# Dense expert pass: the residual parts of the expert weights formed on GpSimd instead of VectorE

## The chip, the cores and the metric

One Trainium2 chip, one of its cores. The metric is the device time of one execution of the whole program in microseconds (us). The engines are named as in the profile: PE (TensorE), DVE (VectorE), ACT (ScalarE), POOL (GpSimd), SP (SyncE, which here only issues transfers).

## The reference

One layer of a diffusion backbone: a mixer (gated MLP and a bidirectional recurrence) and then a channel mixer that picks experts. The change lies in the channel mixer, for 1152 tokens (128 of a prompt, 1024 of a sample), 16384 experts of one neuron each, and 128 chosen experts for each token:

```python
def block(args):
    xb, ib, gb = args
    ue = jnp.take(u_tab, ib, axis=0)
    ve = jnp.take(v_tab, ib, axis=0)
    a = jax.nn.gelu(jnp.einsum('bd,bed->be', xb, ue)) * gb
    return jnp.einsum('be,bed->bd', a, ve)
```

`ib` are the indices of the chosen experts, `gb` their weights (a softmax), `u_tab` and `v_tab` are tables of 16384 rows of 1024 float32. Behind it come a gated residual and a last norm.

## The kernel before

The tokens lie in nine tiles of 128. After the mixer and the choice of experts, two methods share the tiles. Five tiles (640 tokens) are **dense**: they meet every expert, and a weight matrix that is zero for the experts not chosen does the picking. Four tiles are done **row by row**: for each token the rows of its 128 experts are fetched. One of these four is done earlier; the other three go beside the dense pass, as work that fills the engines.

**The dense pass** runs over 128 expert tiles `e` of 128 experts (`for e in range(129)`; its last round only finishes). For each of them:

- SP loads a tile of `u` (`ur`, 128x1024, 512 KB) and one of `v` (`vr`) into one of three buffers with the tag `raw` (`load_split`).
- TensorE multiplies float32 numbers as two parts of a rounded type (float32r): a first part H = round(x), made by ACT as a copy (line 99), and a second part L = x - H, made by DVE as a subtraction (line 100, helper `split`). A product then takes three matmuls: H by H, H by L, L by H (lines 129 to 131, `mmx`). So `ur` becomes `uH`, `uL`, two buffers each, and `vr` becomes `vH`, `vL`, five buffers each.
- `hidden` (lines 977 to 981): 48 matmuls of 320 columns give the activations of the 640 tokens in PSUM (`pH`), and ACT applies the GELU into `a`.
- DVE multiplies `a` by the weights `Gt` (line 1062), and `a` is split into `aH` (ACT) and `aL` (DVE).
- `out_res`: 18 matmuls of 512 columns add this expert tile's part to the sums of three token tiles, which stay in PSUM (`pout`). For the other two token tiles `out_rot` does four expert tiles at a time: 48 matmuls into two PSUM buffers (`prot`, shared with `pH`), and DVE adds each of the four results to a sum in SBUF (`accd`, line 1045).

**The rows** (`gather`): POOL issues an indirect transfer of 128 rows, one for each token of the tile (`gu`, line 795, or `gv`, line 808; 512 KB each), and DVE uses it: line 798 is the product and sum with the token (`jk`), line 813 adds a scaled row to the result (`acc`). The fetched rows have six buffers (four and two more); a fetch waits on POOL until DVE has freed one. 768 rows of this kind (3 tiles, 128 of `u` and 128 of `v` each) are done in the dense pass.

What sets the order: each engine works its instructions off in one order, fixed when the program is built. The rows are advanced from the function `fill`, which stands behind every split and every addition to `accd`: 16 times for four expert tiles, 1.525 rows each time. `anchor` and `paced` keep a row's DVE instruction behind the main stream's instruction that was handed to `fill` two calls ago (`KEEP` = 2). The choice of a tile's experts (`combine_late`, line 119 on DVE) is worked in as well, a little before its rows.

```python
    def paced(ins):
        if anchors:
            tc.add_manual_dep(ins.ins, anchors[0].ins.name,
```

Of the kernel before, what the change touches and what calls it, by code (L numbers as in the profile page):

```python
# [20 lines left out]
NT = 9            # token tiles of 128: tile 0 is the prompt, 1..8 the sample  # L21
NS = 8
EPS = 1e-6
CF = {}           # slots of [128, 512] and of [128, 1024] in the pool of a phase
NGR = 4           # slots of fetched rows, and those that the dense pass adds
# [7 lines left out]
AH = (1, 2)       # of how many blocks of one-hots ScalarE does the weighting  # L33
# [4 lines left out]
TB = 32           # tokens of a block of the weight matrix in DRAM  # L38
OT = 4            # tokens of a block of one-hots
GI = 4            # expert tiles of one load of the weights  # L40
# units of 128 x 1024 weights in the stream
U_ZI, U_HG, U_GR = 0, 4, 16
GATHER = [0, 1, 2, 3]                             # token tiles whose experts are fetched row by row
DENSE = [5, 6, 7, 8, 4]                           # token tiles that meet every expert
ND = len(DENSE)
TD = 128 * ND
RES = 3                                           # dense tiles whose sums stay in PSUM
# [4 lines left out]
def hybrid_kernel(ctx, tc, x_all, pos, c2t, w_ada, b_ada, wst, wspt, bsp, lbraw, vecs, fng, skt, state,  # L52
# [16 lines left out]
    gate_d = dram.tile([4, D], F32, name="gate_d")      # gate1 (ctx, lat), gate2 (ctx, lat)  # L69
# [12 lines left out]
    vec = consts.tile([128, 24], F32, name="vec")        # g1(8) g2(8) sgu(4) hgrn(4), channel on partition  # L82
# [6 lines left out]
    lb = consts.tile([128, 3, 8], F32, name="lb")        # lb, (1-lb)/2, (1+lb)/2  # L89

# [7 lines left out]
    def split(src, H, L):  # L98
        A.activation(H, src, AF.Copy)  # L99
        return V.tensor_tensor(out=L, in0=src, in1=H.bitcast(F32), op=OP.subtract)  # L100
# [3 lines left out]
    def anchor(ins, keep):  # L104
        """the filling work on VectorE queues behind the main stream's instruction `keep` anchors ago"""
        anchors.append(ins)
        while len(anchors) > keep:
            anchors.popleft()
# [15 lines left out]
    def mmx(ps, a, b, first, last):  # L124
        """a.T @ b for operands in one float32 part or in two float32r parts"""
        if len(a) == 1:
            P.matmul(ps, a[0], b[0], start=first, stop=last)
        else:
            P.matmul(ps, a[0], b[0], start=first, stop=False)  # L129
            P.matmul(ps, a[0], b[1], start=False, stop=False)  # L130
            P.matmul(ps, a[1], b[0], start=False, stop=last)  # L131
# [4 lines left out]
    def rap(t, off, dims):  # L136
        """free-dim pattern on a tile"""
        a = t[:]
        return bass.AP(tensor=a.tensor, offset=a.offset + off, ap=[list(a.ap[0])] + dims)

# [9 lines left out]
    # work that fills the engines beside the main stream: generators, advanced a step at a time  # L150
# [42 lines left out]
    # order of the six modulation vectors: shift1 scale1 gate1 shift2 scale2 gate2  # L193
# [30 lines left out]
    def norm_T(pool, xn, which, cnd, parts, back=None):  # L224
        """transposes normalised tiles, applies scale and shift, stores the parts; back(k, full) sees
        the whole float32 value"""
        n = len(xn)
        T = n * 128
        for k in range(8):
            pt = ptp("pnt")  # L230
            for i in range(n):
                P.transpose(pt[:, i * 128:(i + 1) * 128], xn[i][:, k * 128:(k + 1) * 128], ident)
            if len(parts) == 1:
                full = parts[0][:, k, :]
            else:
                full = pool.tile([128, 512], F32, name="full", tag="h512", bufs=CF['h512'])
            A.activation(full[:, 0:T], pt[:, 0:T], AF.Identity, scale=aT[:, which, k, cnd:cnd + 1],
                         bias=modT[:, 2 * which, k, cnd:cnd + 1])
            if len(parts) == 2:
                split(full, parts[0][:, k, :], parts[1][:, k, :])  # L240
            if back is not None:
                back(k, full)
# [25 lines left out]
    def proj_rows(u0, opd, n, evac, native, half=None):  # L268
        """token-major product with a 512 wide block (4 units); opd(k): parts [128, T]; evac(i, psum)"""
# [16 lines left out]
    def hgrn(pool, blocks, proj, vsrc, states):  # L286
        """blocks: (token tile, head) of each 128 columns; proj(j, evac): products for q, fw, bw"""
        NB = len(blocks)
        NTOK = NB * 128
        K2 = pool.tile([128, 2, NTOK], F32, name="K2")       # fw, bw  # L290
        Q2 = pool.tile([128, 2, NTOK], F32, name="Q2")       # bw, fw
        F2 = pool.tile([128, 2, NTOK], F32, name="F2")       # fw, bw
# [27 lines left out]
        for lev in range(7):  # L320
            w = 1 << lev
            Kc = pool.tile([128, NTOK], F32, name="Kc", bufs=1)   # even segments forward, odd ones backward
# [11 lines left out]
            # K: fw first halves by the total of the second, bw second halves by the total of the first  # L334
# [8 lines left out]
            # totals of the doubled segments: the second level in T2, the others in place of the gates  # L343
# [7 lines left out]
        T128 = tbase                                        # F2[:, d, T128 + block]  # L351
# [63 lines left out]
    def combine(gp, t, tv, ti, al=None, c4=None, V=V, h0=0, h1=8, res=None):  # L415
        """the 16 best sums of a head: products of the two lists, with (i+1)(j+1) <= 16"""
# [28 lines left out]
        if res is None:  # L445
            res = al("res", 384).rearrange("p (a b) -> p a b", a=3)    # i1, i2, g
# [3 lines left out]
        hk = lambda x: x[:, :, None, :].to_broadcast(SH)                     # over the list position  # L450
        lp = lambda x: x[:, :, :, None].to_broadcast(SH)                     # over the chosen
# [26 lines left out]
        # softmax over the 16 of a head  # L478
# [16 lines left out]
        else:  # L495
# [3 lines left out]
            rt = gp.tile([128, 2, 128], F16, name="rt", bufs=4)      # i2, i1  # L499
            V.tensor_copy(rt, pt[:, 0:256].rearrange("p (a b) -> p a b", a=2))  # L500
            rg = gp.tile([128, 128], F32, name="rg", bufs=4)         # g (scaled)
            V.tensor_scalar(rg, pt[:, 256:384], 16384.0, None, op0=OP.mult)
            gl = gp.tile([128, 2, 128], F16, name="gl", bufs=4)      # its float16 part, what is left
# [4 lines left out]
    def build_G(gp, i, rt, rg, gl, tags):  # L508
        SH = [128, 2, 128, OT]

        def one_hots(t0):
            o4 = gp.tile([128, 4, 128 * OT], F16, name="oh", tag="c4", bufs=3)
            oh = o4[:, 0:2].rearrange("p a (j t) -> p a j t", t=OT)          # of i2, of i1
            og = o4[:, 2].rearrange("p (t j) -> p t j", t=OT)                # of i1, weighted
# [40 lines left out]
    def group(gp, tiles, hpar, native):  # L555
# [21 lines left out]
        yparts = 2 if tiles is GA else 1                 # the second parts lie where the other group builds  # L577
# [25 lines left out]
        # y_a  # L603
# [32 lines left out]
        # merge, channel on partition (twice the merge: the half goes into the gate)  # L636
# [21 lines left out]
        # out projection and residual  # L658
# [26 lines left out]
        else:  # L685
            advance(choose_q, 10000)
            advance(build_q, 10000)
            # two tiles a part
# [23 lines left out]
        for i in range(n):  # L712
            # the dense tiles wait in DRAM for the dense pass
            if tiles[i] in DENSE:
                c0 = DENSE.index(tiles[i]) * 128
                for z in range(2):
                    for kh in range(2):
                        nc.sync.dma_start(h2T_d[z][:, kh * 4:kh * 4 + 4, c0:c0 + 128],
                                          h2[z].a[kh][:, :, i * 128:(i + 1) * 128].bitcast(F32))
        # queries, scores, top 16 of each half  # L720
# [27 lines left out]
        for i in range(n):  # L748
            t = tiles[i]
            if tiles is GB and t in GATHER:  # L750
                # looked at in the dense pass
# [70 lines left out]
    def final(pool, t, dst, src, x1, gt2, fg):  # L822
        """residual, last norm, store; src: the retrieved sum in column blocks"""
# [12 lines left out]
    # ================= program =================  # L836
# [4 lines left out]
    # left side: a slot for the transposed tokens, and the pool of the row by row retrieval  # L841
# [6 lines left out]
    # lower bound: first row of softmax over the two rows, channel on partition: [128, (dir, head)]  # L848
# [13 lines left out]
    # -- the prompt, token tile 0  # L862
# [42 lines left out]
    # the half of the position embedding that depends on the column is the same for every tile  # L905
# [32 lines left out]
    # -- HGRN over the sample; its tiles in the order of the columns of the two groups  # L938
# [21 lines left out]
    # -- the sample in two groups  # L960
# [21 lines left out]
    # the first expert tiles meet the tokens while the last choice is worked out  # L982
# [23 lines left out]
    def fill(ins):  # L1006
        """fetched rows; the choice of a tile's experts a little before the rows of the one before it end"""
        anchor(ins, KEEP)
# [11 lines left out]
    def load_split(src, nm, bufs):  # L1020
# [3 lines left out]
        fill(split(raw, H, L))  # L1024
# [23 lines left out]
    for e in range(129):  # L1048
        if e < 128:
# [12 lines left out]
            V.tensor_tensor(out=ab, in0=ab, in1=Gt[:, :, e % GI, :], op=OP.mult)  # L1062
# [43 lines left out]
def _layout(ins):  # L1106
    f = lambda n: np.ascontiguousarray(np.asarray(ins[n], dtype=np.float32))

    def tu(w, c0):                   # 128 output channels, all of the contraction: [p, k, 128]
# [3 lines left out]
    def nu(w, c0):                   # 512 output channels as 4 units [p, 2, 512]  # L1113
# [73 lines left out]
```

## Time and profile before

| | |
|---|---|
| runs of the kernel, median of 3 | 3696.43 us (3687.48 to 3701.36) |
| span of the profiled execution | 3697.6 us |
| PE busy | 3351.2 us, 91% |
| PEld (weight loads) | 2757.2 us, 75% |
| DVE busy | 2840.2 us, 77% |
| ACT busy | 1157.4 us, 31% |
| POOL busy | 1440.8 us, 39% |
| mean DMA rate | 263 GB/s over the span |

The profiled execution's own time is known by its span, which is what the sums here are made against; it lies 1.2 us above the median of the runs. The dense pass takes the second half of the span: the first matmul into `pout` starts at 1784 us, the last addition to `accd` at 3675.7 us. In the table a busy share is a mean over all stages; what matters for the change is the share in the dense pass, and how often one engine there waits for another.

### The profile page before, as it was taken

The numbers are of one execution on the slowest core, as the hardware profiler recorded it, in microseconds if no ns is written. First come the engines' busy times: TensorE is split into PE (matmuls) and PEld (weight loads), VectorE is DVE, ScalarE is ACT, GpSimd is POOL, SyncE is SP. The second block draws the span as 40 slices with busy tenths as digits, with TensorE's granted clock in tenths as the row PEclk, the third lists the DMA queues.
The fourth block names the chain that finished last, engine by engine and source line by source line (L and its number), as shares of the span: only waits on it lengthen the run. The fifth ranks groups of instructions, "written<-read, shape, count | busy, mean of one in ns | idle before, by whom it ended". The sixth has DMA issues, their size and how long they took to land. (4 is left out here: it accounts for less than half of the span.)

```text
span 3697.6 us, 48818 instructions
## 1 busy us (share of the span) xinstructions
PE 3351.2 (91%) x17547; PEld 2757.2 (75%) x17547; DVE 2840.2 (77%) x5427; ACT 1157.4 (31%) x2075; POOL 1440.8 (39%) x1128
## 2 busy tenths in 40 slices
PE   7787889899797899888789999889999989999997
PEld 3265678777476676576688989788888878898996
DVE  1315698787499987588787889888888888888888
ACT  2511233432222387735322222222222222222222
POOL 0100632265311220000255554556555465655664
PEclk9899999999898999888799999999999999999998
DMA  7676854488842476441798898889988799989986
GB/s 267 226 272 208 297 189 153 158 292 307 296 161 97 163 278 252 172 165 75 257 327 307 316 335 286 311 298 330 326 308 316 256 327 338 318 301 328 328 313 249
DMA packets 361957, 971.12 MB, mean 263 GB/s; under 512 B 32721, under 2 KB 142673, under 8 KB 356081
## 3 DMA queue, kind: packets, MB, share of 16 engines
q0 software_dynamic: 149824, 546.37, 41.6%
q1 hardware_dynamic: 211888, 421.62, 33.1%
q8 instruction: 138, 2.26, 0.2%
q14 instruction: 107, 0.87, 0.1%
HBM read 897.07 MB, written 70.80 MB: 262 GB/s over the span
## 5 line engine op out<-in xcount | busy, mean ns | idle before, releaser
L795 POOL DMA_INDIRECT gu<-in_urow_dram,ix x512 | 693.5, 1354 | 1024.8 <-DVE jk L798 368.8
L808 POOL DMA_INDIRECT gv<-in_vrow_dram,ix x512 | 694.7, 1357 | 720.6 <-DVE acc L813 388.2
L798 DVE SCALAR_TENSOR_TENSOR jk<-gu,h2r 128x1024 f16<-128x1024 f32 x512 | 624.9, 1220 | 125.0 <-DMA gu<-in_urow_dram,ix 118.7
L813 DVE SCALAR_TENSOR_TENSOR acc<-gv,act,acc 128x1024 f32<-128x1024 f32 x508 | 651.3, 1282 | 65.9 <-DMA gv<-in_vrow_dram,ix 57.9
L129 PE MATMUL pH<-h2DH,uH 128*128 128x320 f32 x2016 | 626.1, 311 | 11.3 <-DVE accd L1045 10.4
L131 PE MATMUL pH<-h2DH,uL 128*128 128x320 f32 x2016 | 623.6, 310 | 3.4 <-DVE uL L100 3.4
L130 PE MATMUL pH<-h2DL,uH 128*128 128x320 f32 x2016 | 624.2, 310 | 0.0
L129 PEld LDWEIGHTS pH<-h2DH,uH 128*128 128x128 f32 x2016 | 380.5, 189 | 21.8 <-DVE accd L1045 15.6
L130 PEld LDWEIGHTS pH<-h2DL,uH 128*128 128x128 f32 x2016 | 380.3, 189 | 4.4
L131 PEld LDWEIGHTS pH<-h2DH,uL 128*128 128x128 f32 x2016 | 380.1, 189 | 4.3 <-DVE uL L100 4.3
L129 PE MATMUL pout<-vH,aH 128*128 128x512 f32 x768 | 298.5, 393 | 22.6 <-ACT vH L99 16.3
L99 ACT ACTIVATE vH<-vr 128x1024 fp32r<-128x1024 f32 x128 | 133.3, 1058 | 561.4 <-DMA vr<-in_vrow_dram 289.4
L130 PE MATMUL pout<-vL,aH 128*128 128x512 f32 x768 | 301.1, 392 | 6.2 <-DVE vL L100 6.2
L131 PE MATMUL pout<-vH,aL 128*128 128x512 f32 x768 | 300.4, 391 | 1.1 <-DVE aL L100 1.0
L129 PE MATMUL prot<-vH,aH 128*128 128x512 f32 x512 | 211.7, 414 | 57.8 <-DVE accd L1045 51.8
L99 ACT ACTIVATE wH<-wraw 128x1024 fp32r<-128x1024 f32 x118 | 125.1, 1060 | 439.4 <-PE pq L130 148.4
L100 DVE TENSOR_TENSOR vL<-vr,vH 128x1024 fp32r<-128x1024 f32 x128 | 156.0, 1220 | 93.7 <-ACT vH L99 93.6
L99 ACT ACTIVATE aH<-a 128x640 fp32r<-128x640 f32 x128 | 94.2, 736 | 368.5 <-DVE a L1062 363.7
L130 PE MATMUL prot<-vL,aH 128*128 128x512 f32 x512 | 208.0, 406 | 0.0
L131 PE MATMUL prot<-vH,aL 128*128 128x512 f32 x512 | 207.3, 405 | 0.0
L99 ACT ACTIVATE uH<-ur 128x1024 fp32r<-128x1024 f32 x126 | 133.4, 1058 | 234.1 <-PE pH L130 214.5
L543 PE MATMUL pG<-oh 128*128 128x128 f16 x1280 | 159.4, 281 | 35.0 <-ACT Gs L546 20.3
(343 smaller groups left out, 6407.7 us busy)
## 6 DMA issues: line engine op xcount, KB each, us to landing
wraw<-in_wst_dram SPq DMA_DIRECT2D x216, 512.0 KB, 4.4
vr<-in_vrow_dram SPq DMA_DIRECT2D x128, 512.0 KB, 6.4
ur<-in_ut_dram SPq DMA_DIRECT2D x126, 512.0 KB, 6.8
G_d<-Gs SPq DMA_DIRECT2D x40, 1024.0 KB, 4.1
Gt<-G_d SPq DMA_DIRECT2D x160, 256.0 KB, 8.7
wraw<-in_w_ada_dram SPq DMA_DIRECT2D x48, 512.0 KB, 4.4
gu<-in_urow_dram,ix POOLq DMA_INDIRECT x512, 6.3
gv<-in_vrow_dram,ix POOLq DMA_INDIRECT x512, 6.9
```

Of the source, the lines that this page charges most:

```text
L99: A.activation(H, src, AF.Copy)
L100: return V.tensor_tensor(out=L, in0=src, in1=H.bitcast(F32), op=OP.subtract)
L129: P.matmul(ps, a[0], b[0], start=first, stop=False)
L130: P.matmul(ps, a[0], b[1], start=False, stop=False)
L131: P.matmul(ps, a[1], b[0], start=False, stop=last)
L543: P.matmul(pg[:, tt * 128:(tt + 1) * 128], oh[:, 0, :, tt], og[a][:, :, tt], start=(a == 0), stop=(a == 1))
L795: G.indirect_dma_start(out=ur, out_offset=None, in_=urow, in_offset=bass.IndirectOffsetOnAxis(ap=ix[:, c:c + 1], axis=0))
L798: paced(V.scalar_tensor_tensor(jk, ur, 1.0, h2r, op0=OP.mult, op1=OP.mult, accum_out=dots[:, k:k + 1]))
L808: G.indirect_dma_start(out=vr, out_offset=None, in_=vrow, in_offset=bass.IndirectOffsetOnAxis(ap=ix[:, c:c + 1], axis=0))
L813: paced(V.scalar_tensor_tensor(acc, vr, act[:, k:k + 1], acc, op0=OP.mult, op1=OP.add))
```

## The change

In `load_split` the subtraction that makes `uL` and `vL` is issued on GpSimd (`G`) instead of VectorE (`V`); `split` gets the engine as an argument, and all its other uses stay on VectorE. The subtraction is no longer an anchor for the rows' DVE work; the product with `Gt` is one now. `fill` is called as often as before, and so the number of rows for an expert tile stays. The rest of the diff takes comments out, and from `split` on most line numbers of the dense pass are one or two higher (1022, 1045, 1054, 1062 become 1023, 1047, 1056, 1064).

```diff
-    def split(src, H, L):
+    def split(src, H, L, E=V):
         A.activation(H, src, AF.Copy)
-        return V.tensor_tensor(out=L, in0=src, in1=H.bitcast(F32), op=OP.subtract)
+        return E.tensor_tensor(out=L, in0=src, in1=H.bitcast(F32), op=OP.subtract)
...
     def fill(ins):
-        anchor(ins, KEEP)
+        if ins is not None:
+            anchor(ins, KEEP)
         k = lates - len(late_q)
...
         H, L = [dp.tile([128, 1024], F32R, name=nm + z, bufs=bufs) for z in "HL"]
-        fill(split(raw, H, L))
+        split(raw, H, L, G)
+        fill(None)
         return H, L
...
-            V.tensor_tensor(out=ab, in0=ab, in1=Gt[:, :, e % GI, :], op=OP.mult)
+            anchor(V.tensor_tensor(out=ab, in0=ab, in1=Gt[:, :, e % GI, :], op=OP.mult), KEEP)
```

The order on POOL in the middle of the pass, before (`gu`, `gv` are fetched rows, `ix` their indices):

```order
L795 DMA gu_17390<-in_urow_dram,ix1_13876 128x1024
L795 DMA gu_17400<-in_urow_dram,ix1_13876 128x1024
L795 DMA gu_17404<-in_urow_dram,ix1_13876 128x1024
L795 DMA gu_17414<-in_urow_dram,ix1_13876 128x1024
L795 DMA gu_17494<-in_urow_dram,ix1_13876 128x1024
L795 DMA gu_17498<-in_urow_dram,ix1_13876 128x1024
L795 DMA gu_17508<-in_urow_dram,ix1_13876 128x1024
```

and the same rows with the change:

```order
L795 DMA gu_17390<-in_urow_dram,ix1_13876 128x1024
L795 DMA gu_17400<-in_urow_dram,ix1_13876 128x1024
L795 DMA gu_17404<-in_urow_dram,ix1_13876 128x1024
L100 TENSOR_TENSOR vL_17411<-vr_17408,vH_17410 128x1024
L795 DMA gu_17414<-in_urow_dram,ix1_13876 128x1024
L795 DMA gu_17494<-in_urow_dram,ix1_13876 128x1024
L795 DMA gu_17498<-in_urow_dram,ix1_13876 128x1024
L100 TENSOR_TENSOR vL_17515<-vr_17512,vH_17514 128x1024
L100 TENSOR_TENSOR uL_17505<-ur_17502,uH_17504 128x1024
L795 DMA gu_17508<-in_urow_dram,ix1_13876 128x1024
```

POOL's queue gets 254 subtractions (128 for `v`, 126 for `u`), mostly one to eight fetches apart, some in pairs; the fetches themselves keep their number.

The order on DVE at the end of one group of four expert tiles, before:

```order
L100 TENSOR_TENSOR uL_17397<-ur_17394,uH_17396 128x1024
L1062 TENSOR_TENSOR a_17145<-a_17145,Gt_17139 128x640
L100 TENSOR_TENSOR aL_17200<-a_17145,aH_17199 128x640
L798 SCALAR_TENSOR_TENSOR jk_17218,dots_17215<-gu_17216,h2r_13878 128x1024
L798 SCALAR_TENSOR_TENSOR jk_17228,dots_17215<-gu_17226,h2r_13878 128x1024
L1045 TENSOR_TENSOR accd0_13757<-accd0_13757,prot_17252 128x512
```

and the same place with the change:

```order
L1064 TENSOR_TENSOR a_17145<-a_17145,Gt_17139 128x640
L813 SCALAR_TENSOR_TENSOR acc_13880<-gv_17203,act_16888,acc_13880 128x1024
L100 TENSOR_TENSOR aL_17200<-a_17145,aH_17199 128x640
L813 SCALAR_TENSOR_TENSOR acc_13880<-gv_17206,act_16888,acc_13880 128x1024
L798 SCALAR_TENSOR_TENSOR jk_17218,dots_17215<-gu_17216,h2r_13878 128x1024
L798 SCALAR_TENSOR_TENSOR jk_17228,dots_17215<-gu_17226,h2r_13878 128x1024
L1047 TENSOR_TENSOR accd0_13757<-accd0_13757,prot_17252 128x512
```

The subtraction of `uL` has left DVE's queue, and a row's instruction now stands between the product with `Gt` and the subtraction of `aL`.

## Rows read from the trace of the kernel before

**Rows 1.** Busy time by engine in the dense pass (windows view)

```profile
core 0: us, PE busy (x) PEld busy (x) DVE busy (x) ACT busy (x) POOL busy (x), PEclk, DMA share, GB/s
1784.00:3676.00 1892.00, 1804.26 (x9888) 1625.04 (x9888) 1579.72 (x2128) 460.75 (x673) 1058.21 (x776) 0.98 0.88 311
```

**Rows 2.** What PE waited for in the dense pass: us in total, times, longest

```profile
PE prot L129 <- DVE accd L1045: 51.8, 16, 9.2
...
PE pH L129 <- DVE accd L1045: 10.4, 5, 6.5
...
PE pout L130 <- DVE vL L100: 6.2, 3, 2.8
...
PE pH L131 <- DVE uL L100: 3.4, 3, 1.7
```

**Rows 3.** Groups of the dense pass by line: busy us, mean ns of one

```profile
L795 POOL DMA_INDIRECT gu<-in_urow_dram,ix x384 | 527.3, 1373 | 653.5 <-DVE jk L798 241.9 <-DMA Gt<-G_d 223.3 <-DVE acc L813 81.7
L808 POOL DMA_INDIRECT gv<-in_vrow_dram,ix x384 | 527.1, 1373 | 347.4 <-DVE acc L813 167.1 <-DVE jk L798 83.2 <-issue 77.9
L813 DVE SCALAR_TENSOR_TENSOR acc<-gv,act,acc 128x1024 f32<-128x1024 f32 x381 | 488.7, 1283 | 27.0 <-DMA gv<-in_vrow_dram,ix 19.7
L798 DVE SCALAR_TENSOR_TENSOR jk<-gu,h2r 128x1024 f16<-128x1024 f32 x384 | 468.7, 1221 | 85.0 <-DMA gu<-in_urow_dram,ix 79.7
...
L100 DVE TENSOR_TENSOR vL<-vr,vH 128x1024 fp32r<-128x1024 f32 x128 | 156.0, 1220 | 93.7 <-ACT vH L99 93.6
L100 DVE TENSOR_TENSOR uL<-ur,uH 128x1024 fp32r<-128x1024 f32 x126 | 153.6, 1220 | 22.1 <-ACT uH L99 21.5 <-DMA vr<-in_vrow_dram 0.5
```

**Rows 4.** What POOL waited for in the dense pass: us, times, longest

```profile
POOL gu L795 <- DVE jk L798: 241.9, 89, 11.9
...
POOL gv L808 <- DVE acc L813: 167.1, 78, 9.6
...
POOL gv L808 <- issue: 77.9, 254, 0.8
POOL gu L795 <- issue: 71.4, 226, 2.0
```

**Rows 5.** Timeline of fetches and row products: start, length, instruction, idle before

```profile
2452.93 0.94 POOL L795 DMA_INDIRECT gu<-in_urow_dram,ix  x1 [0.30 <-issue]
...
2459.26 1.22 DVE L798 SCALAR_TENSOR_TENSOR jk<-gu,h2r 128x1024 f16<-128x1024 f32 x1
...
2459.32 1.98 POOL L795 DMA_INDIRECT gu<-in_urow_dram,ix  x1 [0.30 <-issue]
```

**Rows 6.** Timeline at the end: the same POOL instruction alone and beside DVE

```profile
3678.82 0.19 POOL L94 TENSOR_SCALAR rstd<-ss 128x1 f32<-128x1 f32 x1 [9.83 <-ACT x L831]
3679.09 0.55 POOL L95 TENSOR_TENSOR rstd<-rstd,nhalf 128x1 f32<-128x1 f32 x1
...
3685.21 1.28 DVE L833 SCALAR_TENSOR_TENSOR ftmp<-ftmp,rstd,fgd 128x1024 f32<-128x1024 f32 x1 [0.72 <-POOL rstd L95]
...
3685.26 1.29 POOL L94 TENSOR_SCALAR rstd<-ss 128x1 f32<-128x1 f32 x1
```

**Rows 7.** The longest two-input POOL instruction (groups by line, whole span)

```profile
L95 POOL TENSOR_TENSOR rstd<-rstd,nhalf 128x16 f32<-128x16 f32 x2 | 5.8, 2920 | 0.1
```

**Rows 8.** What DVE waited for in the dense pass: us, times, longest

```profile
DVE vL L100 <- ACT vH L99: 93.6, 35, 7.3
...
DVE aL L100 <- ACT aH L99: 64.7, 72, 2.7
DVE uL L100 <- ACT uH L99: 21.5, 20, 3.7
```

**Rows 9.** What SP's weight loads waited for in the dense pass: us, times, longest

```profile
SPq L1022 <- DVE vL L100: 643.1, 117, 29.6
SPq L1022 <- DVE uL L100: 583.8, 120, 20.1
```

## The prediction, made before the changed kernel was run

> **What bounds the kernel now.** I read the dense pass alone, since nothing outside it changes. First the busy times: of 1892 us PE is busy for 1804, DVE for 1580, and POOL for 1058 [rows 1]. PE leads, and the reader should see how little is left there: 1892 - 1804 = 88 us of idle time, and a granted clock of 0.98, which is worth at most another 0.02 x 1804 = 36 us. So PE's work at full clock needs about 1892 - 88 - 36 = 1768 us. Then the list of what PE waited for: most of its idle time ends with DVE, 51.8 + 10.4 us with the additions to `accd`, 6.2 + 3.4 us with the very subtractions that the change moves [rows 2]. Relieving DVE therefore aims at the right waits, but the prize is at most 88 + 36 = 124 us, 3.4% of the span of 3697.6 us. Next the groups by line and POOL's waits, which show what POOL does: 768 fetches of 1.373 us [rows 3], and between them it waits for DVE to free a row buffer (241.9 and 167.1 us are the largest) [rows 4]. POOL's idle time is real, but it comes in pieces and is not as large as the busy share says: behind most fetches stand 0.31 us that nothing releases (77.9 / 254 and 71.4 / 226) [rows 4].
>
> **Taken from DVE.** 128 + 126 = 254 subtractions of 1.220 us leave [rows 3]: 156.0 + 153.6 = 309.6 us. DVE's busy time in the pass falls from 1580 to about 1270 us. What hid them was nothing but DVE's own slack, so the relief is whole, and DVE's waits for the first parts (93.6 and 21.5 us) leave too [rows 8]. The moved anchor puts a row's product between the multiplication by `Gt` and the subtraction of `aL`, as the order shows; DVE waited there 72 times, 64.7 us in all [rows 8]. This helps DVE a little. It costs nothing, because the number of rows for an expert tile stays, and I take nothing for it either: DVE is no longer what sets the time in my sum.
>
> **Given to POOL.** No row has a subtraction of this size on POOL, so I bound it. From below: the same operation on DVE, 1.220 us [rows 3]. From above: the longest two-input instruction that POOL shows, 2.920 us, a power over 16 columns [rows 7]. The first has the same operands, the second the same engine; neither is nearer, and I take the middle, 2.07 us. The Trainium skill (GPSIMD Engine Reference, "Performance versus the Vector engine") has a two-input float32 operation of 2048 columns at 4497 ns on GpSimd and 2293 ns on VectorE and advises VectorE for such work; half of the first, about 2.25 us, is an estimate from that page for 1024 columns, no run here shows it yet, and by it the sum below would be 46 us longer.
>
> A POOL instruction also waits for DVE. The shortest fetches take 0.94 us; one that started at 2459.32, just behind a row product that ran on DVE until 2460.48, took 1.98 us and ended 0.82 us after that product [rows 5]. At the end of the program the same one-column instruction takes 0.19 us alone and 1.29 us beside a DVE instruction of 1.28 us with two inputs in SBUF [rows 6]. So POOL cannot read SBUF until such a DVE instruction has ended. Over all fetches this costs 1.373 - 0.94 = 0.43 us each, and I charge a subtraction the same. The gap behind a POOL computation is short, 3679.09 - 3678.82 - 0.19 = 0.08 us [rows 6].
>
> **The sum for POOL**, which works in order and has the row fetches queued behind each subtraction:
>
> - now in the pass: 1058 us busy + 768 x 0.31 = 238 us of gaps = 1296 us;
> - 254 x (2.07 + 0.08 + 0.43) = 655 us, together 1951 us;
> - the waits for ACT's first parts, which move with the subtraction from DVE to POOL: 93.6 + 21.5 = 115 us [rows 8]. Behind them now stand fetches and not DVE's main work, but POOL has no time left to make that good. Together 2066 us.
>
> That is 174 us more than the pass lasts. POOL's present waits for row buffers, which filled its time [rows 4], go; POOL itself becomes what is late. Rows then reach DVE later, DVE's queue has the `accd` additions and the products with `Gt` behind the rows, and PE waits for these. Next in line are the loads: SP waits 643.1 + 583.8 us for DVE to free the `raw` buffers [rows 9], and from now on it is POOL that frees them. With three buffers and two loads for an expert tile of some 14.8 us (1892 / 128) a load can come several microseconds late before PE misses it, so I add nothing. The gain of at most 124 us on PE does not come on top, since PE would no longer be what sets the pace.
>
> So: 3697.6 + 174 = 3872 us in the terms of the profiled span, which lies 1.2 us above the median of the runs; I leave it at **3872 us**, 4.7% slower. With the bounds for the subtraction (0.85 us either side, 254 times) the sum moves by 216 us: up to 4088 us, and down to 1850 us for POOL's pass, which is below 1892, so that POOL would just not bind.
>
> **Rivals.**
>
> *VectorE's relief lands and POOL keeps up: faster.* The place is POOL's queue, the price of a subtraction with its gap and waits decides: (1892 - 1296) / 254 = 2.35 us is what POOL has to spare for each, and I charge 2.58 us and 0.45 us for ACT. If fetches no longer met a busy DVE, they would take 0.94 + 0.31 us, 768 of them 960 us, and with 254 x 2.15 = 546 us POOL would end at 1506 us, far below PE. Then PE's waits for DVE go (71.8 us in the four rows [rows 2]) and a part of the lost clock: 3697.6 - 72 = 3626 us, 3574 us at the very best. For it: DVE has 310 us less to do. Against it: its row products stay, they are what fetches wait for, and POOL's subtraction is not free.
>
> *The shared access costs both ways: slower still.* The rows show only POOL waiting for DVE. If POOL's subtraction holds the access in the same way, DVE stands still for 254 x 2.07 = 526 us, its pass becomes 1270 + 526 = 1796 us, and a row product held back goes first when the subtraction ends, so that the next POOL instruction waits for a whole product instead of 0.43 us: 254 x (1.22 - 0.43) = 200 us on POOL's sum, 3872 + 200 = 4072 us. The Trainium skill (SBUF — State Buffer, "Who interferes with whom") says that a VectorE instruction with two SBUF inputs and a GpSimd instruction that reads SBUF exclude each other, whichever starts first, for the whole instruction. By that rule this rival would be the right one; the trace agrees for the half in which POOL waits (0.19 against 1.29 us), and no run yet shows the other half. Against the full price: DVE has idle time (1892 - 1580 = 312 us) in which the subtraction may run and hold back nothing.
>
> *No change that can be measured.* If the subtraction costs 1.4 to 1.6 us, POOL's sum is about as long as the pass, and what DVE gains is used up: 3697 us.
>
> That the change does nothing is excluded: the order has 254 subtractions on POOL and none of them on DVE.
>
> **How the numbers follow.** POOL binds, 3872 us: 0.58. Access both ways, 4072 us: 0.20. No change: 0.09. Faster, 3626 us: 0.13. The first two make it slower, so faster 0.13, same 0.09, slower 0.78, where within 0.5% (18.5 us) counts as the same. The range goes from 3690 us, which takes in no change and leaves the faster case out, to 4090 us, which takes in the bound of 2.92 us and the rival at 4072; what lies above is the two together. I put less than 0.2 outside.
>
> **What would show it.** Right: POOL near 95% busy and waiting in the pass, with its waits for row buffers (`jk`, `acc`) mostly gone; subtractions near 2.1 us on POOL; DVE near 1270 us and waiting for row transfers; PE's idle time above 200 us, with `accd` or `uL` ahead of it. The second rival shows as row products on DVE of well over 1.28 us. Wrong: subtractions under 1.6 us, fetches close to 0.94 us, or PE's idle time under 88 us; then the faster case holds.

## The result, and the profile after

The changed kernel takes 3879.43 us (median of 4 runs, 3873.02 to 3891.09), against 3698.89 us (3687.48 to 3701.54) before: the ratio is 1.0504, 95% interval 1.0477 to 1.0531. It is slower by 5%, 181 us; 3872 us was forecast.

The busy times in the dense pass, which now lasts 2078 us (columns as in [rows 1]), after:

```profile
1771.00:3849.00 2078.00, 1855.64 (x9888) 1660.63 (x9888) 1789.56 (x1870) 460.11 (x674) 1662.77 (x1030) 0.94 0.83 283
```

PE issues the same 9888 matmuls and has 2078 - 1856 = 222 us of idle time in place of 88 [rows 1]. Its busy time is 51 us longer, and the granted clock fell from 0.98 to 0.94: behind idle stretches PE runs at the lower of its two levels (before the change, the first matmuls into `prot` behind an idle stretch of 9.19 us took 0.63 to 0.80 us, later ones 0.39 us). So the pass's 186 us are some 135 us of idle time and 51 us of longer busy time at the lower clock. DVE's busy time did not fall by 310 us, it rose by 210 us, from 1580 to 1790. POOL's rose by 605 us.

What PE waits for in this pass, after:

```profile
PE prot L129 <- DVE accd L1047: 158.5, 30, 11.8
...
PE pH L129 <- DVE accd L1047: 19.2, 6, 8.2
...
PE prot L129 <- DVE accd L1045: 6.9, 1, 6.9
...
PE pout L130 <- POOL vL L100: 1.2, 1, 1.2
```

PE does not wait for the moved subtraction (1.2 us in all). It waits for the additions to `accd` on DVE, 178 us (158.5 + 19.2) in place of 62 (51.8 + 10.4) [rows 2]. The groups by line show what happened to DVE (busy us, mean ns of one), after:

```profile
L798 DVE SCALAR_TENSOR_TENSOR jk<-gu,h2r 128x1024 f16<-128x1024 f32 x384 | 640.7, 1668 | 90.1 <-DMA gu<-in_urow_dram,ix 84.5 <-DVE accd L1047 0.3
L813 DVE SCALAR_TENSOR_TENSOR acc<-gv,act,acc 128x1024 f32<-128x1024 f32 x381 | 640.4, 1681 | 50.4 <-DMA gv<-in_vrow_dram,ix 44.1
...
L808 POOL DMA_INDIRECT gv<-in_vrow_dram,ix x384 | 515.2, 1342 | 153.2 <-issue 76.3 <-DVE acc L813 44.6 <-DVE jk L798 7.9
L795 POOL DMA_INDIRECT gu<-in_urow_dram,ix x384 | 502.6, 1309 | 196.0 <-issue 76.1 <-DVE jk L798 49.4 <-DVE acc L813 30.6
...
L100 POOL TENSOR_TENSOR vL<-vr,vH 128x1024 fp32r<-128x1024 f32 x128 | 325.3, 2542 | 221.6 <-DVE late L119 188.3 <-ACT vH L99 27.7 <-DMA ur<-in_ut_dram 3.5
L100 POOL TENSOR_TENSOR uL<-ur,uH 128x1024 fp32r<-128x1024 f32 x126 | 318.4, 2527 | 11.2 <-ACT uH L99 10.0
...
L1064 DVE TENSOR_TENSOR a<-a,Gt 128x640 f32<-128x640 f32 x127 | 219.9, 1731 | 126.5 <-ACT a L981 120.8 <-ACT uH L99 5.3 <-issue 0.3
...
L1047 DVE TENSOR_TENSOR accd<-accd,prot 128x512 f32<-128x512 f32 x124 | 84.4, 680 | 10.1 <-PE prot L131 10.1
```

The row products went from 1.22 and 1.28 us [rows 3] to 1.67 and 1.68 us in the mean. A minority of them makes this: the median of `jk` stays at 1.22 us, while the longest takes 6.02 us, where it took 1.27 us before. The product with `Gt`, on 640 columns in place of 1024, is longer than either (1.73 us). The additions to `accd`, with one input in SBUF and one in PSUM, take 680 ns, as they did before. These two groups before:

```profile
L1062 DVE TENSOR_TENSOR a<-a,Gt 128x640 f32<-128x640 f32 x126 | 103.1, 818 | 5.6 <-ACT a L981 5.6
...
L1045 DVE TENSOR_TENSOR accd<-accd,prot 128x512 f32<-128x512 f32 x124 | 84.3, 680 | 5.3 <-PE prot L131 5.3
```

The timeline shows it on one piece (start, length, instruction), after:

```profile
2646.23 2.40 POOL L100 TENSOR_TENSOR vL<-vr,vH 128x1024 fp32r<-128x1024 f32 x1
2648.58 2.40 POOL L100 TENSOR_TENSOR uL<-ur,uH 128x1024 fp32r<-128x1024 f32 x1
...
2646.44 5.23 DVE L1064 TENSOR_TENSOR a<-a,Gt 128x640 f32<-128x640 f32 x1 [2.27 <-ACT a L981]
```

The product with `Gt` counts as running from 2646.44, just behind the start of one subtraction, and ends at 2651.67, 0.69 us after the second: it stood still behind both, and did not get in between them. The median of this instruction is 0.82 us. In the profile such a stand-still is no wait; it makes the instruction itself long.

### The profile page after: what moved, and what is told of

It reads as the page before. It is cut to its first block, busy times and chain, and to the rows that moved or that the text cites. A ratio compares the mean times of both kernels' runs of the same rounds, so it can differ in the third digit from the quotient of the medians.

```text
span 3871.2 us, 48967 instructions
## 1 busy us (share of the span) xinstructions
PE 3399.2 (88%) x17547; PEld 2790.6 (72%) x17547; DVE 3050.3 (79%) x5173; ACT 1155.6 (30%) x2075; POOL 2036.8 (53%) x1382
## 5 line engine op out<-in xcount | busy, mean ns | idle before, releaser
L795 POOL DMA_INDIRECT gu<-in_urow_dram,ix x512 | 662.8, 1294 | 571.7 <-DVE jk L798 174.8
L808 POOL DMA_INDIRECT gv<-in_vrow_dram,ix x512 | 681.4, 1331 | 522.9 <-DVE acc L813 258.2
L798 DVE SCALAR_TENSOR_TENSOR jk<-gu,h2r 128x1024 f16<-128x1024 f32 x512 | 796.9, 1556 | 126.0 <-DMA gu<-in_urow_dram,ix 118.0
L813 DVE SCALAR_TENSOR_TENSOR acc<-gv,act,acc 128x1024 f32<-128x1024 f32 x508 | 803.0, 1581 | 86.1 <-DMA gv<-in_vrow_dram,ix 78.8
L129 PE MATMUL pH<-h2DH,uH 128*128 128x320 f32 x2016 | 627.8, 311 | 24.2 <-DVE accd L1047 19.2
L100 POOL TENSOR_TENSOR vL<-vr,vH 128x1024 fp32r<-128x1024 f32 x128 | 325.3, 2542 | 221.6 <-DVE late L119 188.3
L129 PE MATMUL prot<-vH,aH 128*128 128x512 f32 x512 | 230.5, 450 | 166.9 <-DVE accd L1047 158.5
L1064 DVE TENSOR_TENSOR a<-a,Gt 128x640 f32<-128x640 f32 x128 | 220.7, 1724 | 141.4 <-ACT a L981 120.8
L100 POOL TENSOR_TENSOR uL<-ur,uH 128x1024 fp32r<-128x1024 f32 x126 | 318.4, 2527 | 11.2 <-ACT uH L99 10.0
L129 PEld LDWEIGHTS prot<-vH,aH 128*128 128x128 f32 x512 | 111.4, 218 | 205.4 <-DVE accd L1047 171.5
L130 PE MATMUL prot<-vL,aH 128*128 128x512 f32 x512 | 222.8, 435 | 0.0
```

The costliest lines, as they stand in the source:

```text
L100: return E.tensor_tensor(out=L, in0=src, in1=H.bitcast(F32), op=OP.subtract)
L795: G.indirect_dma_start(out=ur, out_offset=None, in_=urow, in_offset=bass.IndirectOffsetOnAxis(ap=ix[:, c:c + 1], axis=0))
L798: paced(V.scalar_tensor_tensor(jk, ur, 1.0, h2r, op0=OP.mult, op1=OP.mult, accum_out=dots[:, k:k + 1]))
L808: G.indirect_dma_start(out=vr, out_offset=None, in_=vrow, in_offset=bass.IndirectOffsetOnAxis(ap=ix[:, c:c + 1], axis=0))
L813: paced(V.scalar_tensor_tensor(acc, vr, act[:, k:k + 1], acc, op0=OP.mult, op1=OP.add))
L1064: anchor(V.tensor_tensor(out=ab, in0=ab, in1=Gt[:, :, e % GI, :], op=OP.mult), KEEP)
```

## The experiments

Two theories were open. **POOL's queue binds** (my forecast): the subtractions fill POOL, rows come late. **DVE stands still** (my second rival): what counts is that DVE cannot run while POOL reads SBUF. Ratios are to the kernel before, run on the same chips; 0.01 of it is 37 us. Edits are shown against the changed kernel, where nothing else is said.

**One part alone: only the anchor.**

```diff
-        split(raw, H, L, G)
+        split(raw, H, L)
```

> The subtraction back on VectorE, everything else as in the change (the product with Gt is an anchor, the subtraction is none). Both theories (GpSimd's queue binds; VectorE stands still behind the subtraction) put the whole loss into the place of the subtraction: 3699 us as before the change, at best 65 us less if the row products that now stand between the product with Gt and the subtraction of aL fill VectorE's waits there. A time near 3879 us would say that the moved anchor did the harm.

Measured: 3662.01 us, ratio 0.9906 (0.9890 to 0.9922). So the change consists of two parts of opposite sign: the anchor gives 0.9% back, and the place of the subtraction costs 1.0504 - 0.9906 = 0.0598, some 221 us. This kernel beats both; PE's waits for `accd` are 32.5 us there (19.7 + 12.8), in place of 62.2 us [rows 2].

**Half of the subtractions.**

```diff
-        split(raw, H, L, G)
+        split(raw, H, L, G if nm == "u" else V)
```

> Only the 126 subtractions for u on GpSimd, the 128 for v on VectorE. GpSimd's queue binds: its sum falls by 128 x 2.5 = 320 us to about 1530 us, far below the pass, so no loss, 3650 to 3720 us. VectorE stands still: half of the loss stays, 3780 to 3800 us, with about half as many long row products.

Measured: 3767.91 us, ratio 1.0193 (1.0170 to 1.0216), outside both forecasts and nearer to the second. Against the kernel with the anchor alone that is 0.0287, 48% of the 0.0598, although POOL, in a pass of 1971 us, is busy for no more than 1329 us (fifth pair of the row, columns as in [rows 1]):

```profile
1771.00:3742.00 1971.00, 1821.23 (x9888) 1632.42 (x9888) 1697.23 (x2009) 464.02 (x675) 1329.32 (x902) 0.97 0.87 300
```

The row products are longer too, by 137 us in all, in place of 324 us with all subtractions on POOL:

```profile
L813 DVE SCALAR_TENSOR_TENSOR acc<-gv,act,acc 128x1024 f32<-128x1024 f32 x381 | 562.3, 1476 | 35.6 <-DMA gv<-in_vrow_dram,ix 30.3 <-DVE acc L813 0.2
L798 DVE SCALAR_TENSOR_TENSOR jk<-gu,h2r 128x1024 f16<-128x1024 f32 x384 | 532.3, 1386 | 56.4 <-DMA gu<-in_urow_dram,ix 51.7
```

Half of the subtractions make half of the loss, with POOL busy for two thirds of the pass; a queue that binds only when full would not do that.

**POOL as busy, without reading SBUF.** The second part of the expert weights is left out of the products.

```diff
-        split(raw, H, L, G)
+        A.activation(H, raw, AF.Copy)
+        for _ in range(3):
+            G.memset(L.bitcast(F32), 0.0)
```

> In place of each subtraction GpSimd writes zeros over the second part, three times, and reads nothing in SBUF; so the second part of the expert weights is left out of the products. GpSimd is as busy as with the subtractions (some 2.4 us each if one write takes 0.8 us). GpSimd's queue binds: 3850 to 3900 us as with the change. VectorE stands still: row products back at 1.22 to 1.28 us, the time at or below that before the change, 3600 to 3700 us.

Measured: 3721.04 us, ratio 1.0068 (1.0048 to 1.0088). One write takes 0.97 us, so three are longer than a subtraction, and the time lies outside both forecasts, though far nearer to the second. Writes of 731 us in all, more than the 644 us of the subtractions, cost 0.0278 of the time (1.0068 - 0.9790) against a kernel without a subtraction (below). The next run matches the length (edit against the one just shown):

```diff
-        for _ in range(3):
-            G.memset(L.bitcast(F32), 0.0)
+        for c in (1024, 1024, 512):
+            G.memset(L[:, 0:c].bitcast(F32), 0.0)
```

> As the write-only kernel, but two and a half writes in place of three (2 x 0.97 + 0.49 = 2.4 us, the length of the subtraction, 2.41 us), the second part of the expert weights left out again. GpSimd's occupancy alone: if 2.91 us for each cost 3721 - 3618 = 103 us, 2.43 us should cost 50 to 100 us: 3670 to 3715 us. What then lies between it and 3879 us is VectorE standing still, 165 to 210 us of the 261 us between the change and the kernel without a subtraction.

Measured: 3656.28 us, ratio 0.9917 (0.9904 to 0.9930). That is 14 us below the range: I had priced occupancy too high. The groups by line of this kernel:

```profile
L813 DVE SCALAR_TENSOR_TENSOR acc<-gv,act,acc 128x1024 f32<-128x1024 f32 x381 | 488.7, 1283 | 148.3 <-DMA gv<-in_vrow_dram,ix 142.5 <-DVE accd L1049 0.9
...
L798 DVE SCALAR_TENSOR_TENSOR jk<-gu,h2r 128x1024 f16<-128x1024 f32 x384 | 469.3, 1222 | 165.8 <-DMA gu<-in_urow_dram,ix 159.9 <-issue 1.8 <-DVE accd L1049 0.4
...
L1027 POOL MEMSET vL<- 128x1024 f32 x252 | 244.8, 972 | 2.6 <-PE prot L130 2.5
...
L1027 POOL MEMSET uL<- 128x1024 f32 x248 | 241.0, 972 | 15.8 <-PE pH L131 15.5
...
L1027 POOL MEMSET vL<- 128x512 f32 x127 | 68.9, 543 | 0.1
L1027 POOL MEMSET uL<- 128x512 f32 x125 | 68.1, 545 | 0.1
```

POOL writes for 623 us, against 644 us of subtractions in the change, and DVE's row products are back at their old 1.22 and 1.28 us, the longest `jk` at 1.27 us. What is left of occupancy shows as DVE's waits for rows (142.5 + 159.9 us), which PE does not feel much: it waits 23 us for `accd`. In the change these waits for rows are only 44.1 + 84.5 us, so rows come less late there, and yet PE loses more. Two things differ besides the reading: a write does not wait for ACT's first part, and the `raw` buffer is free once ACT has read it, so loads may start earlier here. The next run has the second of these back, not the first.

**POOL reading one input.** In place of the second part stands the whole weight (edit against the kernel of the matched writes).

```diff
-            G.memset(L[:, 0:c].bitcast(F32), 0.0)
+            G.tensor_copy(L[:, 0:c], raw[:, 0:c])
```

> As the matched write-only kernel, but GpSimd copies the raw tile (one input read in SBUF) in place of writing zeros, two and a half tiles for each subtraction; the second part is then the whole weight, so the products are not the reference's. If reading is what makes VectorE stand still: long row products (mean over 1.5 us) and 3850 to 3950 us at equal length of the GpSimd work. If two inputs are needed for that: like the matched writes, 3670 to 3715 us.

Measured: 3991.61 us, ratio 1.0816 (1.0801 to 1.0831). Groups by line of this kernel:

```profile
L813 DVE SCALAR_TENSOR_TENSOR acc<-gv,act,acc 128x1024 f32<-128x1024 f32 x381 | 642.1, 1685 | 148.6 <-DMA gv<-in_vrow_dram,ix 142.4 <-issue 1.4
L798 DVE SCALAR_TENSOR_TENSOR jk<-gu,h2r 128x1024 f16<-128x1024 f32 x384 | 635.5, 1655 | 189.4 <-DMA gu<-in_urow_dram,ix 186.0
...
L1027 POOL CAST vL<-vr 128x1024 fp32r<-128x1024 f32 x256 | 321.0, 1255 | 199.2 <-DMA vr<-in_vrow_dram 194.3 <-PE prot L130 4.5
...
L1027 POOL CAST uL<-ur 128x1024 fp32r<-128x1024 f32 x252 | 290.2, 1152 | 1.1
...
L1027 POOL CAST uL<-ur 128x512 fp32r<-128x512 f32 x126 | 114.4, 908 | 0.4
...
L1027 POOL CAST vL<-vr 128x512 fp32r<-128x512 f32 x128 | 104.2, 814 | 0.5
```

One input read in SBUF is enough: the row products are as long as in the change. The time lies above the forecast range, which was meant for equal length. The length is not equal, since three copies wait for DVE three times (830 us on POOL with the half tiles, not 644), so the extra over the change is not the reading's alone: DVE waits 142.4 + 186.0 us for rows, more than in the change, and PE 33.6 us for `uL`.

**Shorter pieces.**

```diff
-        split(raw, H, L, G)
+        A.activation(H, raw, AF.Copy)
+        for c in range(0, 1024, 256):
+            s = slice(c, c + 256)
+            G.tensor_tensor(out=L[:, s], in0=raw[:, s], in1=H[:, s].bitcast(F32), op=OP.subtract)
```

> The subtraction on GpSimd in four pieces of 256 columns (about 0.65 us each). If the length of one stand-still makes the loss (accd held up behind a long one), VectorE gets in between the pieces and the time falls, 3780 to 3850 us. If the sum of GpSimd's SBUF time makes it, the pieces cost more, since each waits for VectorE anew: 3900 to 4000 us.

Measured: 4154.53 us, ratio 1.1262 (1.1232 to 1.1292). Groups by line of this kernel:

```profile
L813 DVE SCALAR_TENSOR_TENSOR acc<-gv,act,acc 128x1024 f32<-128x1024 f32 x381 | 618.1, 1622 | 172.4 <-DMA gv<-in_vrow_dram,ix 167.7
L798 DVE SCALAR_TENSOR_TENSOR jk<-gu,h2r 128x1024 f16<-128x1024 f32 x384 | 594.7, 1549 | 211.5 <-DMA gu<-in_urow_dram,ix 206.9
L1028 POOL TENSOR_TENSOR vL<-vr,vH 128x256 fp32r<-128x256 f32 x512 | 537.8, 1078 | 218.9 <-DVE late L119 190.1 <-ACT vH L1025 26.6
L1028 POOL TENSOR_TENSOR uL<-ur,uH 128x256 fp32r<-128x256 f32 x504 | 522.7, 1065 | 2.2 <-ACT uH L1025 1.2
```

and its busy times (columns as in [rows 1]):

```profile
1771.00:4102.00 2331.00, 1896.34 (x9888) 1688.52 (x9888) 1641.74 (x1882) 459.61 (x675) 1997.81 (x1792) 0.90 0.74 253
```

That is above both forecasts. A piece takes 1.07 us, four of them 4.3 us where one whole subtraction took 2.5. The shortest pieces take 0.71 us, so some 1.4 of the 4.3 us are POOL's waits for DVE. DVE's row products are hardly shorter (1.62 and 1.55 us). But DVE is busy for 1642 us in this pass, less than in the change (1790), and waits 167.7 + 206.9 us for rows, while POOL is busy for 1998 us of 2331: the further loss goes with rows that come late from a longer POOL queue, the mechanism that I had forecast for the change itself. This is read from the busy times; no run separates it.

**No subtraction at all.** The first part stands in for the second; the residual of the weights is left out.

```diff
-        H, L = [dp.tile([128, 1024], F32R, name=nm + z, bufs=bufs) for z in "HL"]
-        split(raw, H, L, G)
+        H = dp.tile([128, 1024], F32R, name=nm + "H", bufs=bufs)
+        A.activation(H, raw, AF.Copy)
         fill(None)
-        return H, L
+        return H, H
```

> No subtraction on any engine: the first part stands in for the second in the products (the residual of the expert weights is left out). What the relief of VectorE is worth when nothing takes its place: 3626 us by PE's waits for VectorE, 3574 us if the clock is full as well. Both theories say the same here. If it stays near 3699 us, there was nothing to gain at all.

Measured: 3618.20 us, ratio 0.9790 (0.9775 to 0.9805). Its busy times (columns as in [rows 1]):

```profile
1771.00:3594.00 1823.00, 1780.78 (x9888) 1616.97 (x9888) 1292.53 (x1883) 461.34 (x677) 962.61 (x778) 0.99 0.92 324
```

This is what relief alone can give: 2.1%, and nearly half of that comes with the anchor. DVE's busy time is 1293 us, close to the 1270 us that I had forecast for the change.

**Which part of the anchor.** The subtractions as anchors again, with the product with `Gt` as one more:

```diff
-        split(raw, H, L, G)
-        fill(None)
+        fill(split(raw, H, L))
```

> The kernel before with the product with Gt as one more anchor (the subtractions on VectorE stay anchors): 20 anchors for four expert tiles in place of 16, so row products are held back less. The kernel with the subtraction as no anchor was at 3662 us. If the new anchor made that gain, this one has it too: 3655 to 3670 us; if it was the subtraction's being no anchor, about 3699 us.

Measured: 3688.84 us, ratio 0.9994 (0.9980 to 1.0008): no gain. And neither of the two as an anchor:

```diff
-        split(raw, H, L, G)
+        split(raw, H, L)
...
-            anchor(V.tensor_tensor(out=ab, in0=ab, in1=Gt[:, :, e % GI, :], op=OP.mult), KEEP)
+            V.tensor_tensor(out=ab, in0=ab, in1=Gt[:, :, e % GI, :], op=OP.mult)
```

> The kernel before with the subtraction of the weights as no anchor, and the product with Gt none either: 8 anchors for four expert tiles. If it is the subtraction's being no anchor that gave 3662 us, this one lies there too, 3655 to 3675 us; if it took both edits together (the product with Gt as anchor alone gave 3689 us, no change), about 3699 us.

Measured: 3663.74 us, ratio 0.9918 (0.9899 to 0.9937), as with the change's anchors. It is the subtraction's being no anchor that gains; the new anchor does nothing that can be seen.

**Further in that direction.** `KEEP` at 3 and at 4, with the subtraction on VectorE:

```diff
-KEEP = 2
+KEEP = 3
```

> The subtraction on VectorE with the anchors of the change (3662 us) and a row product held back only behind the third last anchor instead of the second last. If fewer and further anchors help because row products can fill VectorE's waits for ACT, some of the 44 us between 3662 us and the kernel without a subtraction (3618 us) comes: 3640 to 3662 us. If row products then stand ahead of accd and hold it up, 3662 to 3720 us.

Measured: 3679.05 us, ratio 0.9954 (0.9937 to 0.9971).

> As the one with the third last anchor, with the fourth last: further in the same direction, 3640 to 3740 us; it tells whether a gain goes on or turns.

Measured: 3702.76 us, ratio 1.0021 (1.0003 to 1.0039). The gain turns: PE's waits for `accd` at `prot` are 37.7 and 59.4 us here, 19.7 us with `KEEP` at 2. So 2 is best of the three, and 3662 us the best complete kernel of this study.

**The account.** In parts of the time before: anchor -0.0094; no subtraction on VectorE -0.0116 (0.9790 - 0.9906); POOL occupied for as long +0.0127 (0.9917 - 0.9790); POOL reading SBUF meanwhile +0.0587 (1.0504 - 0.9917), some 217 us. Relief and occupancy cancel within the intervals; what comes with the reading is the loss.

## Why the prediction was right, and where it was not

The time, the sign and the range were right: 3872 us forecast, 3879 measured. The mechanism that I gave the greater chance was not the cause, so the nearness of the number is luck.

- *PE leads and the prize is small*: right. At most 124 us of prize were read from PE's idle time and clock, 72 us from its waits for DVE; without any subtraction the kernel gains 0.021 of the time before, 78 us, the anchor included.
- *DVE falls to about 1270 us*: the step that failed first. It does where nothing takes the subtraction's place (1293 us). In the change it is 1790 us. Three kinds of DVE instruction that I priced as before are longer by 172 (`jk`: 640.7 - 468.7), 152 (`acc`) and 116 us (`Gt`, against a median of 0.82 us each), together 440 us, more than the 310 us that left. I had read that POOL waits for DVE [rows 5, 6] and left the other direction to a rival.
- *The second rival*, access that costs both ways, is what happens, and the sign that I named for it came: row products of 1.67 and 1.68 us, well over 1.28. Its DVE figure, 1796 us, stands against 1790, in part by luck: the subtractions are longer than the 2.07 us that I multiplied, and DVE was held for 520 us (1790 - 1270) of their 644. Its price was wrong, since I set it on top of POOL's sum (4072 us) where it replaces it. The rule of the Trainium skill (SBUF — State Buffer, "Who interferes with whom") agrees with each run here on which instructions hold each other up: row products long beside a subtraction or a copy, and unchanged beside pure writes; additions with one SBUF input unchanged at 680 ns. Whether the one that starts first is also the one that runs, as the prediction cites it, can't be read from the starts in the profile (last section).
- *The subtraction at 2.07 us*: mis-sized. The median is 2.41 us, the mean with its wait 2.53. The estimate of 2.25 us from the Trainium skill (GPSIMD Engine Reference, "Performance versus the Vector engine") was nearer, and still short. The wait that I charged, 0.43 us, is about 0.12, so the two together (2.50 and 2.53 us) came out right by accident.
- *Waits for ACT move with it, 115 us*: 27.7 + 10.0 us on POOL.
- *POOL binds, 2066 us*: it does not. It is busy for 1663 us of 2078 (80%, not 95), has some 152 us of gaps between, and still waits for DVE to free row buffers, as this list shows for the change:

```profile
POOL gv L808 <- issue: 76.3, 274, 0.3
POOL gu L795 <- issue: 76.1, 275, 0.6
POOL gu L795 <- DVE jk L798: 49.4, 34, 4.0
POOL gv L808 <- DVE acc L813: 44.6, 36, 2.8
```

  The two waits for `jk` and `acc` were 241.9 and 167.1 us [rows 4]. Their shrinking is what I named as a sign that POOL binds, and it is not one: with the matched writes, which occupy POOL alike, they are smaller still (19.5 and 28.3 us), and the occupancy costs 47 us, less than the relief of DVE and the anchor give.
- *The moved anchor costs and gives nothing*: wrong by 0.94%, 35 us. I looked at the new anchor, which is worth nothing; the one taken away is what counts.
- *Loads may come late without PE missing them*: right. SP's waits grew to 943.6 us for `vL` and 644.9 us for `uL`, now on POOL, where DVE had freed the buffers [rows 9], and PE waited 1.2 us for these tiles.
- *PE's idle time above 200 us with `accd` ahead of it*: right, 222 us, 178 of them behind the additions. They stand behind row products in DVE's queue, whichever mechanism makes those late, and so did not tell the two apart.

That POOL's sum of 2066 us fell on the pass's 2078 us is chance. Two terms of it were too high: ACT's waits by 77 us, and the gaps by 86 us, since 768 of them were charged (238 us) and 549 show (152 us). POOL's work, its gaps and its waits for ACT come to 1663 + 152 + 38 = 1853 us; most of the rest of the pass it waits for DVE. What stays open is how much of the 217 us is the later release of the `raw` buffers and POOL's wait for ACT, which the pure writes lack. PE waited 1.2 us for the second parts of `v`, and for the first parts as long as with the matched writes (15.9 and 16.0 us, once each), so it should be little, but no run has it alone.

## What to carry to other kernels

Before an operation goes from VectorE to GpSimd, look at what VectorE does beside it: where that has two inputs in SBUF, as here, it can be held for as long as GpSimd reads. Here an operation of 1.22 us became one of 2.41 us, which took 310 us off VectorE and put 520 us on. GpSimd's idle share says nothing on this; the test is a GpSimd instruction of the same length that only writes. And separate a change's parts: here an anchor that gained 0.9% sat inside a change that lost 5%.

## What was not expected of the hardware

A blocked VectorE instruction appears in the profile as a long one (the product with `Gt`: median 0.82 us, longest 5.99 us) and not as a wait, so busy time rose where work had left. Nor does the earlier start in the profile always win: that longest product starts at 2594.64, 0.55 us ahead of a subtraction that stands right behind a fetch on GpSimd, and ends at 2600.63, behind that subtraction and the next. Two subtractions in a row kept VectorE out for both (4.75 us from the first start to the last end), with nothing let in between. A subtraction cut into four cost 4.3 us in place of 2.5, of which some 1.4 us is GpSimd waiting for VectorE anew.
